# A new order for the head of a two-layer decoder trunk, and another buffer pool for the operands that return at its turn

## The chip, the cores and the metric

One core of one Trainium2 chip runs the whole program. The metric is the device time of one execution in microseconds (us). Before the change the median of three runs is 1879.58 us (1879.56 to 1881.36); one more execution was profiled.

## The reference, cut to what matters

The input x has 2048 rows of 1024 features, p has two layers of 2048 rows of 256. Everything is float32.

```
h = x
for i in (0, 1):
    hn = rmsnorm(h, norm_mix[i])
    if i == 0:                       # gated short convolution, 1024 -> 4 x 1024
        b, c, v, z = split(hn @ a_w_in)
        h += (silu(z) * b * conv3(c * v)) @ a_w_out
    else:                            # gated causal window means over 2, 4, 8, 16 rows
        u, z = split(hn @ b_w_in)
        d = window_means(u) - u      # by groups of 256 features
        h += (silu(z) * (d @ w_grp) * scale) @ b_w_out
    gate = sigmoid(rmsnorm(h, ple_norm[i]) @ ple_w_gate[i])
    h += gate * (p[i] @ ple_w_proj[i])      # the embedding projection
return rmsnorm(h, final_norm)
```

## The kernel before, in words

The rows are cut into four chunks of 512, and features lie on the 128 partitions, eight tiles of 128 by 512 to a chunk. Each float32 factor is split into a high and a low part (the split: a ScalarE cast, line 108 for weights and 240 for operands, and a VectorE subtraction, lines 109 and 241), and each product is three matmuls (lines 212 to 214, `mm`).

Weights come in granules of 128 by 1024 (512 KB). `order` (from line 160) lists all granules in the order of their use; `next_granule` hands out the next one and `prefetch` loads and splits those that lie a few places ahead (one in the head, three later). A granule is loaded into one of four buffers of pool `rawp` and split into one of four buffers of `wring`, or, for p and its projections and the group weights, into two tiles of the token pool `acts` (28 tiles of 128 by 2 by 512). Pool `hp` has ten tiles of 128 by 512 for the chunk that is worked on, pool `wk` ten work tiles for everything short-lived. PSUM has seven banks for products.

The first mixer (`mixer_a`, `pair_steps`) works on two chunks at once with a seven-product scheme in place of eight: its operands x11, x21, t2, t1, t3, x22 and t4, four tiles each, are norms, sums and differences of the two chunks' x. For each output pair of weights it takes x11 and x21 (24 matmuls of 128 by 512), then t2 and t1, then t3 and x22, then t4.

*The head* (from line 725). Some matmuls on constants run first. Then `load_chunk`, `square_sums` and `roots` prepare the norms of chunks 0 and 1, `fold_next` multiplies the group weights into the second mixer's input weights (four folds of 48 matmuls of 128 by 256, stored to DRAM as `wcomb`, each half fold through a buffer of `rawp`), and `ple(0, (0, 1))`, as the last call before the mixer, projects the embeddings of chunks 0 and 1 (96 matmuls) and stores them to DRAM (`p_dram`), from where the gate reads them later.

*The turn.* After the second chunk (`turn`), the mixer needs the operands of chunks 2 and 3. `prepare(kk)` builds those of two feature tiles ahead of time and stores them to DRAM (`n_dram`); the four calls are spread over the work on chunk 1. `second_operand` (line 529) loads one tile back and splits it into the token pool; `Operands.ahead(n)` does so for the next n of the 28.

All loads and stores are issued by SP, in one queue. The program is written in one order, but a planner with its own estimates of durations sets the final order of each engine's instructions: it takes the earliest written one that its estimate finds ready. On the chip each engine then runs its instructions strictly in that order.

Of the kernel before, what the change touches and what calls it, by code (L numbers as in the profile page):

```python
# [9 lines left out]
F32 = mybir.dt.float32  # L10
# [5 lines left out]
P = 128  # L16
D = 1024
S = 2048
T = 512
KT = D // P  # L20
NCH = S // T
# [12 lines left out]
W_GATE = (40, 50)  # L34
W_BZ = 60
W_BOUT = 68
# [11 lines left out]
def trunk_kernel(ctx: ExitStack, tc: tile.TileContext, xT, xN, pT, wts, par, out):  # L48
    nc = tc.nc
# [4 lines left out]
    acts = ctx.enter_context(tc.tile_pool(name="acts", bufs=28))  # L54
    hp = ctx.enter_context(tc.tile_pool(name="hp", bufs=10))
# [8 lines left out]
    def wtile():  # L64
        return wk.tile([P, 528], F32, tag="wk", name="wk")
# [29 lines left out]
    p_dram = {key: dram.tile([P, KT, T], F32, name=f"pdr{key[0]}{key[1]}", tag=f"pdr{key[0]}{key[1]}") for key in PLE_EARLY}  # L95
# [64 lines left out]
    order = []  # L160
# [10 lines left out]
    def ple_order(layer, ch, halves):  # L171
        return [("p", layer * NCH + ch)] + [("pt", W_GATE[layer] + 8 + h) for h in halves]

    for g in range(4):
        order += [("pt", W_GRP + g // 2)] if g % 2 == 0 else []
        order += [("w", W_UT + 2 * g), ("w", W_UT + 2 * g + 1)]
    order += ple_order(0, 0, (0,)) + ple_order(0, 1, (1,))
    for ch in range(NCH):
        if ch % 2 == 0:
            order += [("sum", (0, 0)), ("sum", (1, 0))]  # L180
# [13 lines left out]
    pos = [0]  # L194
    look = [LOOK]

    def prefetch(upto):
        while len(loaded) < len(order) and len(loaded) <= upto:
            loaded.append(load_granule(order[len(loaded)]))

    def next_granule(key):
        prefetch(pos[0] + look[0])
        assert order[pos[0]] == key, (order[pos[0]], key)
        w = loaded[pos[0]]
        pos[0] += 1
        return w


    def mm(ps, w, col, act, first, last, skip=False):
        wh, wl = w[0][:, col:col + P], w[1][:, col:col + P]  # L210
        ah, al = act
        nc.tensor.matmul(out=ps, lhsT=wh, rhs=ah, start=first, stop=False, skip_group_check=skip)  # L212
        nc.tensor.matmul(out=ps, lhsT=wh, rhs=al, start=False, stop=False, skip_group_check=skip)  # L213
        nc.tensor.matmul(out=ps, lhsT=wl, rhs=ah, start=False, stop=last, skip_group_check=skip)  # L214
# [6 lines left out]
    def psum():  # L221
        return pm.tile([P, T], F32, tag="mm", name="mm")
# [154 lines left out]

    def pair_steps(i, X):

        pa, pb = psum(), psum()  # L380
        w = next_granule(("sum", (i, 0)))
        product(pa, w, 0, X("x11"), True)
        product(pb, w, HK, X("x21"), True)
        c1 = copied(pa)
# [142 lines left out]
        nc.sync.dma_start(out=n_dram[kk][:, 5:7, :], in_=b)  # L527

    def second_operand(name, kk):
        n = wtile()[:, :T]  # L530
        nc.sync.dma_start(out=n, in_=n_dram[kk][:, SLOT[name], :])
        return split_act(n)

# [47 lines left out]
    def mixer_out(base, ys, hs, layer, extra=nop):  # L581
        s = Stat()
        a = []
        for k in range(KT):
            ps = dense(("w", base + k), ys)
            nc.vector.tensor_tensor(out=hs[k], in0=ps, in1=hs[k], op=ALU.add)  # L586
            a.append(split_scaled(hs[k], G_PLE + 8 * layer + k))
            s.add(hs[k], nc.vector if k == KT - 1 else nc.gpsimd)
            extra(k)
        return a, s  # L590
# [11 lines left out]
               i == 0, i == 1)  # L602
        return g_ps, p_ps

    def ple(layer, chs):

        pts, wps = {}, []
        base = W_GATE[layer] + 8
        for h in range(2):
            if h < len(chs):  # L610
                pts[chs[h]] = next_granule(("p", layer * NCH + chs[h]))
            wps.append(next_granule(("pt", base + h)))
        for h in range(2):
            for ch in chs:
                pt = pts[ch]
                for k in range(4 * h, 4 * h + 4):
                    ps = psum()
                    for i in range(2):
                        mm(ps, wps[h], ((k % 4) * 2 + i) * P,
                           (pt[0][:, i * T:(i + 1) * T], pt[1][:, i * T:(i + 1) * T]), i == 0, i == 1)  # L620
                    e = wtile()[:, :T]
                    nc.scalar.copy(out=e, in_=ps)
                    nc.sync.dma_start(out=p_dram[layer, ch][:, k, :], in_=e)

    def gate_out(g_ps, p_ps, h, rb, c0, c1):
        t = wtile()[:, :c1 - c0]
# [108 lines left out]
    x, stats = [], []  # L735

    def load_chunk(t):
        x.append([])
        for k in range(KT):
            xt = hp.tile([P, T], F32, tag="h", name="x") if t * KT + k < 10 else wtile()[:, :T]  # L740
            nc.sync.dma_start(out=xt, in_=xT[t, :, k, :])
            x[t].append(xt)

    def square_sums(t):
        s = Stat()
        for k in range(KT):
            s.add(x[t][k], nc.vector)
        stats.append(s)

    def roots(t):  # L750
        stats[t].fin1()
        stats[t].fin2()
# [3 lines left out]
    def fold_next(g):  # L756
        if g % 2 == 0:
            wg.append(next_granule(("pt", W_GRP + g // 2)))
        fold(g, wg[-1], [next_granule(("w", W_UT + 2 * g + c)) for c in range(2)])

    prefetch(2)
    load_chunk(0)
    square_sums(0)
    fold_next(0)
    load_chunk(1)
    roots(0)
    fold_next(1)
    square_sums(1)
    X = Operands(first_operand(x, stats))
    X("x11")  # L770
    fold_next(2)
    roots(1)
    X("x21")
    fold_next(3)
    X("t2")
    ple(0, (0, 1))


    sums_n = const.tile([P, 8], F32, name="sums_n")
    rbs = []  # L780
# [12 lines left out]
    def preparing(kk):  # L793
        return lambda k: prepare(kk, rbs) if k == KT - 1 else None

    for sc in range(2):
        ya = mixer_a(sc, X)
        ys = [split_act(y) for y in ya]
        for t in range(2):
            ch = 2 * sc + t  # L800
            more = ch + 1 < NCH
            turn = (sc, t) == (0, 1)
            hs = load_x(ch)
            a, s = mixer_out(W_AOUT, ys, hs, 0)
            a, s = gate(0, ch, a, hs, s, G_MIX + 8, preparing(1) if turn else nop)
            ys = mixer_b(ch, a, s, gather if ch == 0 else preparing(2) if turn else nop)
            if (1, ch) in PLE_EARLY:
                ple(1, (ch,))
            a, s = mixer_out(W_BOUT, ys, hs, 1, preparing(3) if turn else nop)
            if not more:  # L810
                look[0] = 1
                gate_last(1, ch, a, hs, s)
                break
            nys = []
            if turn:
                X = Operands(second_operand)

            def ahead(k):
                if turn:
                    X.ahead(3 if k < KT - 1 else 2)  # L820
                    return
                nys.append(later_half(sc, k))
                if ch == 0 and k == KT - 1:
                    prepare(0, rbs)

            _, s = gate(1, ch, a, hs, s, None, ahead)
            hooks.extend(finals(ch, hs, s))
            ys = nys
# [53 lines left out]
```

## Time and profile before

| | before |
|---|---|
| median of runs | 1879.58 us |
| profiled execution | 1880.67 us |
| its span | 1878.9 us |
| TensorE busy | 1815.6 us, 97% |
| VectorE busy | 1304.8 us, 69% |
| ScalarE busy | 755.2 us, 40% |
| GpSimd busy | 253.5 us, 13% |
| moved by DMA | 223.75 MB, 119 GB/s in the mean |

All times inside the program are counted from the start of the span. In the profile, PE is TensorE, DVE is VectorE, ACT is ScalarE, POOL is GpSimd and SPq is the queue of SyncE, which issues the transfers. "PEclk" is the granted clock of TensorE, where 1.00 is 2.4 GHz and 0.50 is 1.2 GHz.

### The profile page before, as it was taken

To read this page: it belongs to the slowest core of one execution; us is meant where nothing else is said; L and a number is where in the kernel's file an instruction comes from. 1 tells how busy PE (TensorE), PEld (TensorE's weight loads), DVE (VectorE), ACT (ScalarE), POOL (GpSimd) and SP (SyncE) were. 2 spreads that over 40 slices of the span, in tenths; PEclk is the share of its full clock that TensorE was granted. 3 is DMA by queue.
4 is the path that set the end of the run, shared out by engine and by line. 5 is a ranking of instruction groups with operands and counts; after the bars stand their busy time and mean duration, and the time that the engine had idled before them with its cause. 6 is when DMAs were issued, how large, how long until landed. Compare 5 with 4: busy or idle time off the path is not lost.

```text
span 1878.9 us, 21641 instructions
## 1 busy us (share of the span) xinstructions
PE 1815.6 (97%) x8189; PEld 1503.2 (80%) x8189; DVE 1304.8 (69%) x1791; ACT 755.2 (40%) x1100; POOL 253.5 (13%) x233
## 2 busy tenths in 40 slices
PE   7699999999999999999978999999999999999997
PEld 5587888888888888888856888888888888888897
DVE  7856665765796667896677675666668666768665
ACT  6633333344444434434353233334433344443332
POOL 1000000002221122211110000000222112120010
PEclk7899999999999999999988999999999999999998
DMA  7611111243343455536543111114322343622221
GB/s 252 236 62 64 55 62 62 68 158 123 129 158 123 135 174 191 185 101 207 201 168 113 62 62 62 62 68 162 123 90 90 102 134 113 202 78 92 99 90 45
DMA packets 77272, 223.75 MB, mean 119 GB/s; under 512 B 8560, under 2 KB 10608, under 8 KB 77168
## 3 DMA queue, kind: packets, MB, share of 16 engines
q1 hardware_dynamic: 77168, 222.38, 34.8%
q8 instruction: 64, 1.05, 0.2%
q14 instruction: 40, 0.33, 0.1%
HBM read 191.93 MB, written 30.41 MB: 118 GB/s over the span
## 4 chain that ended last, share of the span: by engine, by line
PE 91%; DVE 3%; DMA 2%; ACT 2%; issue 1%; SPq 0%; POOL 0%; DVEq 0%; ACTq 0%
PE mm L212 30%; PE mm L214 30%; PE mm L213 30%; DVE w L109 1%; DMA wk<-ndr 1%; DMA raw<-in_wts_dram 1%; ACT w L108 1%; DVE act L241 0%; PE tot L280 0%; ACT wc L359 0%; DMA wcomb<-wc 0%; ACT wk L267 0%; DVE h L661 0%; DMA wk<-in_xT_dram 0%; DVE wk L629 0%
## 5 line engine op out<-in xcount | busy, mean ns | idle before, releaser
L212 PE MATMUL mm<-act,w 128*128 128x512 f32 (+1 forms) x2560 | 975.1, 385 | 26.1 <-ACT w L108 8.2
L213 PE MATMUL mm<-act,w 128*128 128x512 f32 (+1 forms) x2560 | 981.6, 384 | 0.2 <-DVE act L241 0.2
L214 PE MATMUL mm<-act,w 128*128 128x512 f32 (+1 forms) x2560 | 966.2, 384 | 3.0 <-DVE w L109 2.9
L212 PEld LDWEIGHTS mm<-act,w 128*128 128x128 f32 x2560 | 487.1, 190 | 129.0 <-ACT w L108 12.1
L108 ACT CAST w<-raw 128x1024 fp32r<-128x1024 f32 (+1 forms) x296 | 296.7, 1006 | 678.5 <-PE mm L214 439.3
L213 PEld LDWEIGHTS mm<-act,w 128*128 128x128 f32 x2560 | 487.0, 190 | 94.2 <-DVE act L241 1.2
L214 PEld LDWEIGHTS mm<-act,w 128*128 128x128 f32 x2560 | 482.0, 189 | 98.6 <-DVE w L109 5.1
L109 DVE TENSOR_TENSOR w<-raw,w 128x1024 fp32r<-128x1024 f32 (+1 forms) x296 | 346.5, 1173 | 130.6 <-ACT w L108 129.8
L270 POOL TENSOR_TENSOR acc<-acc,wk 128x512 f32<-128x512 f32 x97 | 148.9, 1535 | 568.3 <-ACT wk L267 568.0
L375 DVE TENSOR_TENSOR wk<-mm,wk 128x512 f32<-128x512 f32 x96 | 66.0, 689 | 153.7 <-PE mm L214 151.6
L586 DVE TENSOR_TENSOR h<-mm,h 128x512 f32<-128x512 f32 x64 | 43.4, 688 | 80.1 <-PE mm L214 77.0
L247 DVE SCALAR_TENSOR_TENSOR act<-h,par_sb,act 128x512 fp32r<-128x512 f32 x96 | 92.5, 973 | 7.6 <-ACT act L246 7.5
L246 ACT ACTIVATE act<-h,par_sb 128x512 fp32r<-128x512 f32 x96 | 69.1, 719 | 64.7 <-DVE h L630 46.8
L267 ACT ACTIVATE wk<-h 128x512 f32<-128x512 f32 (+1 forms) x119 | 70.9, 596 | 50.9 <-DVE h L630 49.4
L370 ACT COPY wk<-mm 128x512 f32<-128x512 f32 x96 | 52.5, 581 | 88.1 <-PE mm L214 88.1
L240 ACT CAST act<-wk 128x512 fp32r<-128x512 f32 x82 | 49.7, 619 | 69.7 <-DVE wk L577 46.1
L241 DVE TENSOR_TENSOR act<-wk,act 128x512 fp32r<-128x512 f32 x82 | 58.4, 719 | 26.5 <-ACT act L240 26.5
L212 PE MATMUL mm<-act 128*128 128x512 f32 (+1 forms) x144 | 53.5, 374 | 15.3 <-ACT act L108 15.3
L627 DVE TENSOR_TENSOR wk<-mm,rb 128x512 f32<-128x512 f32 (+1 forms) x72 | 44.3, 626 | 34.5 <-PE mm L214 24.8
L423 POOL COPY wk<-uh 128x2 f32<-128x2 f32 x16 | 14.1, 882 | 362.4 <-DVE wk L375 285.6
L109 DVE TENSOR_TENSOR w<-s,w 128x1024 fp32r<-128x1024 f32 x32 | 39.8, 1243 | 28.4 <-ACT w L108 28.2
L560 DVE TENSOR_TENSOR wk<-wk 128x512 f32<-128x512 f32 (+5 forms) x80 | 55.4, 693 | 2.1
(111 smaller groups left out, 1223.0 us busy)
## 6 DMA issues: line engine op xcount, KB each, us to landing
raw<-in_wts_dram SPq DMA_DIRECT2D x252, 512.0 KB, 3.3
raw<-wcomb SPq DMA_DIRECT2D x32, 512.0 KB, 3.3
h<-in_xT_dram SPq DMA_DIRECT2D x32, 256.0 KB, 5.3
wk<-ndr SPq DMA_DIRECT2D x28, 256.0 KB, 4.9
pdr<-wk SPq DMA_DIRECT2D x24, 256.0 KB, 3.1
wk<-pdr SPq DMA_DIRECT2D x24, 256.0 KB, 4.0
out_dram<-h SPq DMA_DIRECT2D x24, 256.0 KB, 2.8
wcomb<-wc SPq DMA_DIRECT2D x16, 256.0 KB, 4.3
```

Of the source, the lines that this page charges most:

```text
L108: nc.scalar.copy(out=hi[:, c], in_=raw[:, c])
L109: eng.tensor_tensor(out=lo[:, c], in0=raw[:, c], in1=hi[:, c].bitcast(F32), op=ALU.subtract)
L212: nc.tensor.matmul(out=ps, lhsT=wh, rhs=ah, start=first, stop=False, skip_group_check=skip)
L213: nc.tensor.matmul(out=ps, lhsT=wh, rhs=al, start=False, stop=False, skip_group_check=skip)
L214: nc.tensor.matmul(out=ps, lhsT=wl, rhs=ah, start=False, stop=last, skip_group_check=skip)
L241: nc.vector.tensor_tensor(out=a[:, 1, :], in0=y, in1=a[:, 0, :].bitcast(F32), op=ALU.subtract)
L246: nc.scalar.activation(out=a[:, 0, :], in_=h, func=AF.Copy, scale=pcol(gcol))
L247: nc.vector.scalar_tensor_tensor(out=a[:, 1, :], in0=h, scalar=pcol(gcol), in1=a[:, 0, :].bitcast(F32), op0=ALU.mult, op1=ALU.subtract)
L267: nc.scalar.activation(out=sq, in_=h, func=AF.Square)
L270: (eng or nc.gpsimd).tensor_tensor(out=acc, in0=acc, in1=sq, op=ALU.add)
L375: nc.vector.tensor_tensor(out=o, in0=ps, in1=c, op=ALU.add)
L560: nc.vector.tensor_tensor(out=nxt[:, lo:end], in0=cur[:, lo:end], in1=cur[:, lo - step:end - step], op=ALU.add)
```

## The change

The head is rewritten: the embedding projections run first, then the four folds and the operands between them. The list of granules is put in the same order. `ple` takes one chunk, and the second call uses the projections of the first again. The second chunk of x is loaded as four transfers of two tiles into the token pool instead of eight transfers into `hp` and `wk`. Loads are called for by `prefetch` at written places.

At the turn, `second_operand` loads into `hp` instead of `wk`. The first four returns are asked for in the stage before (`mixer_out`, tiles 4 to 7), then two in place of three for each tile of the gate. The last `prepare` is called after tile 3 instead of tile 7.

```diff
@@ order
+    order += ple_order(0, 0, (0, 1)) + ple_order(0, 1, ())
     for g in range(4):
         order += [("pt", W_GRP + g // 2)] if g % 2 == 0 else []
         order += [("w", W_UT + 2 * g), ("w", W_UT + 2 * g + 1)]
-    order += ple_order(0, 0, (0,)) + ple_order(0, 1, (1,))
@@ second_operand
-        n = wtile()[:, :T]
+        n = hp.tile([P, T], F32, tag="h", name="nx")
         nc.sync.dma_start(out=n, in_=n_dram[kk][:, SLOT[name], :])
         return split_act(n)
@@ ple
-    def ple(layer, chs):
...
+    def ple(layer, ch, wps=None):
+
+        pt = next_granule(("p", layer * NCH + ch))
+        wps = wps or [next_granule(("pt", W_GATE[layer] + 8 + h)) for h in range(2)]
+        for k in range(KT):
+            ps = psum()
+            for i in range(2):
+                mm(ps, wps[k // 4], ((k % 4) * 2 + i) * P,
+                   (pt[0][:, i * T:(i + 1) * T], pt[1][:, i * T:(i + 1) * T]), i == 0, i == 1)
+            e = wtile()[:, :T]
+            nc.scalar.copy(out=e, in_=ps)
+            nc.sync.dma_start(out=p_dram[layer, ch][:, k, :], in_=e)
+        return wps
@@ load_chunk
-        for k in range(KT):
-            xt = hp.tile([P, T], F32, tag="h", name="x") if t * KT + k < 10 else wtile()[:, :T]
-            nc.sync.dma_start(out=xt, in_=xT[t, :, k, :])
-            x[t].append(xt)
+        for k in range(0, KT, 2):
+            if t == 0:
+                pair = [hp.tile([P, T], F32, tag="h", name="x") for _ in range(2)]
+                for i in range(2):
+                    nc.sync.dma_start(out=pair[i], in_=xT[t, :, k + i, :])
+            else:
+                both = acts.tile([P, 2, T], F32, tag="act", name="x2")
+                nc.sync.dma_start(out=both, in_=xT[t, :, k:k + 2, :])
+                pair = [both[:, i, :] for i in range(2)]
+            x[t].extend(pair)
@@ head
     prefetch(2)
     load_chunk(0)
+    prefetch(3)
     square_sums(0)
-    fold_next(0)
+    ple(0, 1, ple(0, 0))
+    prefetch(6)
     load_chunk(1)
     roots(0)
-    fold_next(1)
+    fold_next(0)
     square_sums(1)
     X = Operands(first_operand(x, stats))
     X("x11")
+    fold_next(1)
+    X("x21")
+    roots(1)
     fold_next(2)
-    roots(1)
-    X("x21")
     fold_next(3)
+    prefetch(pos[0] + 1)
     X("t2")
-    ple(0, (0, 1))
@@ main loop
             if (1, ch) in PLE_EARLY:
-                ple(1, (ch,))
-            a, s = mixer_out(W_BOUT, ys, hs, 1, preparing(3) if turn else nop)
+                ple(1, ch)
+            if turn:
+                X = Operands(second_operand)
+
+            def before(k):
+                if turn and k == 3:
+                    prepare(3, rbs)
+                if turn and k > 3:
+                    X.ahead(1)
+
+            a, s = mixer_out(W_BOUT, ys, hs, 1, before)
...
-            if turn:
-                X = Operands(second_operand)
-
             def ahead(k):
                 if turn:
-                    X.ahead(3 if k < KT - 1 else 2)
+                    X.ahead(2)
                     return
```

## Rows read from the trace of the kernel before

**Rows 1.** The page: share of the span, and 40 slices of it in tenths.
```profile
PE 1815.6 (97%) x8189; PEld 1503.2 (80%) x8189; DVE 1304.8 (69%) x1791; ACT 755.2 (40%) x1100; POOL 253.5 (13%) x233
...
PEclk7899999999999999999988999999999999999998
```

**Rows 2.** Timeline of TensorE in the head: start us, duration us, line, tiles.
```profile
12.84 0.28 PE L212 MATMUL mm<-act,w 128*128 128x256 f32 x1
12.96 0.28 PE L213 MATMUL mm<-act,w 128*128 128x256 f32 x1
...
76.93 0.39 PE L212 MATMUL mm<-act 128*128 128x512 f32 x1
77.16 0.39 PE L213 MATMUL mm<-act 128*128 128x512 f32 x1
...
92.12 0.39 PE L212 MATMUL mm<-act,w 128*128 128x512 f32 x1
```

**Rows 3.** Windows of the head: length, busy us (instructions) by engine, clock, DMA share.
```profile
33.30:45.00 11.70, 9.18 (x41) 8.89 (x42) 11.70 (x18) 6.75 (x14) 0.00 (x0) 0.50 0.23 75
...
6.40:97.10 90.70, 62.53 (x316) 54.76 (x317) 78.47 (x114) 59.99 (x114) 4.44 (x3) 0.79 0.69 239
...
92.10:121.60 29.50, 29.50 (x132) 24.41 (x131) 13.39 (x20) 8.29 (x14) 0.84 (x2) 1.00 0.24 83
```

**Rows 4.** Groups of TensorE by line and shape, 0 to 121.6 us.
```profile
L212 PE MATMUL mm<-act,w 128*128 128x256 f32 x64 | 21.5, 350 | 5.5 <-ACT w L108 4.8 <-ACT wc L359 0.7
```

**Rows 5.** Waits, 0 to 170 us: us in total, times, longest us.
```profile
PE mm L212 <- ACT act L108: 15.3, 1, 15.3
```

**Rows 6.** Windows before and in the turn, columns as in rows 3.
```profile
892.00:957.00 65.00, 65.00 (x288) 53.76 (x287) 46.28 (x62) 27.27 (x40) 11.02 (x7) 1.00 0.56 194
957.00:1030.00 73.00, 54.42 (x193) 41.03 (x192) 54.72 (x83) 29.35 (x48) 7.73 (x8) 0.84 0.39 137
```

**Rows 7.** Waits of TensorE, 880 to 1060 us.
```profile
PE mm L212 <- ACT wk L370: 6.9, 1, 6.9
PE mm L212 <- ACT act L240: 5.9, 2, 4.6
```

**Rows 8.** Timeline of VectorE: the last operand splits of the head.
```profile
95.14 1.89 DVE L241 TENSOR_TENSOR act<-x,act 128x512 fp32r<-128x512 f32 x3
```

**Rows 9.** Waits of SP's queue, 0 to 100 us.
```profile
SPq L102 <- DMA wcomb<-wc: 10.1, 4, 4.3
```

**Rows 10.** Timeline of SP's queue in the turn.
```profile
973.42 0.32 SPq L643 DMA_DIRECT2D wk<-pdr  x1
...
992.61 0.33 SPq L102 DMA_DIRECT2D raw<-in_wts_dram  x1
992.99 2.32 SPq L531 DMA_DIRECT2D wk<-ndr  x5
```

**Rows 11.** Timeline of ScalarE in the turn.
```profile
982.01 0.63 ACT L267 ACTIVATE wk<-h 128x512 f32<-128x512 f32 x1 [2.39 <-DVE h L630]
982.54 1.05 ACT L370 COPY wk<-mm 128x512 f32<-128x512 f32 x2
```

**Rows 12.** The page: costliest groups (busy, mean ns), then transfers (count, KB, us to landing).
```profile
L108 ACT CAST w<-raw 128x1024 fp32r<-128x1024 f32 (+1 forms) x296 | 296.7, 1006 | 678.5 <-PE mm L214 439.3
L109 DVE TENSOR_TENSOR w<-raw,w 128x1024 fp32r<-128x1024 f32 (+1 forms) x296 | 346.5, 1173 | 130.6 <-ACT w L108 129.8
L240 ACT CAST act<-wk 128x512 fp32r<-128x512 f32 x82 | 49.7, 619 | 69.7 <-DVE wk L577 46.1
L241 DVE TENSOR_TENSOR act<-wk,act 128x512 fp32r<-128x512 f32 x82 | 58.4, 719 | 26.5 <-ACT act L240 26.5
...
raw<-in_wts_dram SPq DMA_DIRECT2D x252, 512.0 KB, 3.3
...
wk<-ndr SPq DMA_DIRECT2D x28, 256.0 KB, 4.9
```

**Rows 13.** Waits of SP's queue, 900 to 1030 us.
```profile
SPq L102 <- DVE w L109: 75.4, 11, 16.0
```

More of the change, by code (lines that the diff above doesn't have):

```diff
@@ L603, in gate_mm @@
         return g_ps, p_ps
-    def ple(layer, chs):
[L607 to L623, printed above, removed]
+    def ple(layer, ch, wps=None):
[10 more added lines that the diff above has]
+        return wps
     def gate_out(g_ps, p_ps, h, rb, c0, c1):
```

## The prediction, on record before the changed kernel ran

> **What bounds the kernel now.** I read the busy shares first, then the row of 40 slices, then the causes of TensorE's idle time, then the two stretches that they point to. TensorE is busy 97% of the span, and its granted clock is full but for the first slices and one place in the middle [rows 1]. So the kernel is a stream of matmuls, 0.2267 us from the start of one 128x512 matmul to the next (76.93 to 77.16 and on, [rows 2]), and a change can only win where that stream is broken: in the head (0 to 92 us) and at the turn between the halves of the sequence (957 to 1030 us). The diff touches just these.
>
> Head. The mixer's first matmul runs at 92.12 us [rows 2], and behind it the stream is whole: 29.5 us from there hold 29.50 us of busy TensorE [rows 3]. Before it TensorE has 192 fold matmuls (64 on each of three lines, [rows 4]) at 0.12 us (12.84 to 12.96, [rows 2]), 23.0 us; 96 embedding matmuls (2 chunks x 8 tiles x 2 halves x 3) at 0.2267, 21.8 us; and some 1.4 us of statistics, 46.2 us in all. The first fold starts at 7.7 us, so an unbroken head would end at 53.9 us: 38.2 us are lost. The largest piece is one wait of 15.3 us [rows 5], for the cast of an embedding granule, which stands behind the folds and finds no early slot; the others are 3 to 4 us each. The rest is clock: from 33.3 to 45 us, after such gaps, the granted clock is 0.50 [rows 3], the 1.2 GHz level.
>
> Turn. A full stream records 288 matmuls in 65 us (892 to 957); the 73 us behind it hold 193 where 323 would fit [rows 6]. The missing 130, at 65/288 = 0.226 us, are 29.3 us lost, 18.6 us of it idle (73 less 54.42) and the rest a lower clock (0.84 in the mean). Two waits of TensorE lead: 6.9 us for a PSUM copy, 5.9 us for operand casts [rows 7].
>
> **The change, part by part.**
>
> Order of the head. The embeddings come first and need only p and its projections, so TensorE can start at the same 7.7 us: the first three granules have the size of those that stood there. 21.8 us of matmuls, and some 1.5 us for a half clock at the start as the first fold had it, lead to 31 us; beside them run the casts of the fold weights, the squares of x and the first roots. The 15.3 us wait goes, since its granules are the first loaded. Late next is VectorE. From 6.4 to 97.1 us it was busy 78.5 us, 87% [rows 3], and its last operand splits end at 97.0 [rows 8]. None of that work is removed: granule splits, 14 square adds, norms, sums, 28 operand splits. The last operand, t4, is wanted 96 matmuls after the mixer's first (two steps of 24 on x11 and x21, then 12 each on t2, t1, t3, x22), 21.8 us later. If VectorE never waits, t4 is done at 6.4 + 78.5 = 84.9 and the mixer can start, in effect, at 63.1 us, a gain of 29 us. At the old 87%, t4 stays at 97.0 and the start is 75.2, a gain of 17. I take the middle, 69 us, since granule work now covers VectorE's early waits for x while the roots' chain through TensorE and GpSimd stays: gain 23 us. The lower bound: the folds now stand directly in front of the mixer, and each half fold keeps one of four raw buffers until its store has landed, for which weight loads already stood 10.1 us on SP [rows 9]. If that is paid in full on top of the old 87%, the gain is 7 us. The DMA engines were 69% busy in the same stretch [rows 3]; at full load its bytes take 63 us, to 69 us, no later than VectorE.
>
> Loads of x. Chunk 1 comes as four transfers of 512 KB in place of eight of 256 KB, in the token pool of 28 in place of pools h and wk, which leaves all ten work tiles to the embeddings' evictions. These 16 stores move to the front of SP's queue, ahead of fold weights: at 0.32 to 0.46 us an issue (as SP's rows show, [rows 10]) 5 to 7 us, hidden under 21.8 us of embedding matmuls. Without that cover the fold waits those 7 us; four fewer loads give 1.5 us back at best. I take nothing for both.
>
> The turn. The returning operands leave the work tiles, for which the gate's temporaries and its embedding tiles compete. The gate's last embedding tile was loaded only at 973.42 us [rows 10], 16 us into the stretch that should hold the mixer, and the PSUM copy for which TensorE waited 6.9 us ran on ScalarE at 982.54 behind a square that itself waited for the gate's tail [rows 11]. With this competition gone, and x11 fetched one stage ahead, I expect both waits to go, 12.8 us, with half of the 10.7 us of lower clock, 5: 17.8 us. Against it stand the new buffers. Pool h has ten, eight hold the chunk, so two returns fly at a time. One takes 4.9 us to land, 0.62 us of cast and 0.72 us of subtraction [rows 12], 6.24 us, so 3.12 us a return. Twenty of 28 can be back before the gate's own operands free the token pool: from 893 us that is 955 us, in time. The last eight (x22, t4) need four rounds, 25 us, to 980 and beyond, where before five came in one burst at 992.99 [rows 10]. They are wanted from 19 us after the mixer's start at 957 on, 976 to 979; the burst's replacement is then some 8 us late and I take that in full: net gain 10 us. Bounds: 29 us gained if nothing is left of the loss; if the 17.8 do not come and two rounds more are waited for, 12 us lost.
>
> Preparing the fourth operand pair at tile 3 in place of 7 moves two loads, eight VectorE passes and four stores into a stretch in which VectorE is busy 46 of 65 us [rows 6]. It leaves the way between the last sum and the root, but TensorE did not stop for that root: nothing; under 1 us either way, a pass at the most. The projection of the second layer issues what it issued: nothing.
>
> Sum: 1880.7 us (span 1878.9 and 1.8 around it) - 23 - 10 = 1847.7; the profiled run lies 1.1 us above the median of the runs, so 1847 us beside them.
>
> **Rivals.** (1) VectorE gives the head back. For it: it is 87% busy over the whole head. Against: in the old order the mixer began 5 us before the last split was ready, 17 us later than it need have. Head 7, turn 3 gained: 1870 us. (2) Two buffers starve the turn: 3.12 us a return is above the 2.72 us (12 matmuls) at which two per gate tile are asked, and any queueing on VectorE adds to each round. Against: x11 starts a stage earlier. Head 23 gained, turn 5 lost: 1862 us. (3) Slower: SP's one queue at the turn. A return that waits for its buffer stands before the weight loads. SP already stood up to 16.0 us for a weight buffer [rows 13], and the five returns behind that load were issued 0.4 us after it, at 992.99 [rows 10]. If a tile's two returns must first free a buffer and the next weights land only after, a tile takes 6.2 us and 5.5 us more (landing 3.3, cast 1.0, split 1.2, [rows 12]), 11.7 in place of 5.44 us: 50 us on eight tiles, less 16 us that three granules of look-ahead cover, 34 us lost. With a head of 23 and none of the 10 it ends at 1892 us. It decides from the point where a buffer wait exceeds 5.44 us a tile; against it, 3.12 us a return is near the pace asked. The Trainium skill (DMA: Bandwidth & Descriptors, Anatomy of one DMA) says that DMA engines wait on no semaphore and that any such wait is on the issuing sequencer, before dispatch; by that rule this queueing is certain wherever a buffer is late, and the 0.4 us above agrees. (4) The planner, which orders each queue by its own estimate of times, gives the written order away and the moved lines issue where they did: 1880 us.
>
> **How the numbers follow.** Forecast 0.58, own range 1836 to 1859; rival 1, 0.18; rival 2, 0.11; rival 3, 0.08; rival 4, 0.05. About 0.2% (3.8 us) is what a measurement of this kernel tells from no change. Faster: forecast and rivals 1 and 2, 0.87; same 0.05; slower 0.08. The range of 8 in 10 takes in rival 2, most of rival 1 and a little of a turn that loses nothing more: 1834 to 1872.
>
> **What would show it.** The first embedding matmul at 7.7 us; no idle TensorE above 5 us before the mixer; its first matmul between 58 and 75 us, with some gaps behind it put down to VectorE (t2, t1, t4). At the turn no wait for the PSUM copy, the gate's embedding loads 5.4 us apart, and short waits for casts at x22 and t4. I am wrong if the mixer starts as early as that but TensorE then idles over 15 us for splits, or if SP's weight loads wait on buffers of h.

## The result, and the profile after

The changed kernel takes 1857.37 us (median of 4 runs, 1856.24 to 1859.52) beside 1879.57 us of the kernel before on the same chip: a ratio of 0.9882, 95% interval 0.9865 to 0.9899, so 22.2 us are gained where 33 were forecast. Its profiled execution has 1859.5 us and a span of 1857.7.

To see where the 21.2 us of span come from I align the two traces on an instruction that both have: ScalarE's copy of the row factor for a later norm. Lines of its timeline (start us, duration us, engine and line, tiles, idle before and releaser), the kernel before, then after:

```profile
463.72 0.59 ACT L303 COPY rb<-bc 128x512 f32<-128x512 f32 x1 [1.86 <-PE bc L301]
...
1352.88 0.59 ACT L303 COPY rb<-bc 128x512 f32<-128x512 f32 x1 [0.27 <-PE bc L301]
```

```profile
458.88 0.59 ACT L303 COPY rb<-bc 128x512 f32<-128x512 f32 x1 [1.86 <-PE bc L301]
...
1332.01 0.59 ACT L303 COPY rb<-bc 128x512 f32<-128x512 f32 x1 [0.27 <-PE bc L301]
```

The first pair lies behind the head and before the turn, the second behind both. The changed kernel is 4.84 us ahead at the first and 20.87 at the second. So **the head gained 4.8 us and the turn 16.0**, where I had written 23 and 10. Below, "head" and "turn" of a run are these two differences against the kernel before. They come from one execution each: two heads of the same code differ by up to 2 us (4.84 here, 6.68 in e7, which has the same head).

From the page of the changed kernel, the granted clock in 40 slices of the span:

```profile
PEclk9889999999999999999999999999999999999998
```

The dip of the clock in the middle is gone, the one at the start has only become smaller [rows 1]. The head in windows, columns as in [rows 3], and the turn's window as in [rows 6]:

```profile
6.40:65.00 58.60, 47.73 (x256) 41.70 (x257) 41.26 (x57) 42.90 (x81) 4.02 (x3) 0.91 0.77 283
65.00:105.00 40.00, 26.64 (x112) 21.63 (x111) 39.79 (x61) 21.98 (x40) 0.00 (x0) 0.79 0.44 141
17.50:40.50 23.00, 23.00 (x135) 20.30 (x133) 13.27 (x18) 18.11 (x35) 1.65 (x1) 1.00 0.97 361
957.00:1030.00 73.00, 65.64 (x270) 52.90 (x269) 57.30 (x83) 26.82 (x41) 9.14 (x9) 0.93 0.31 106
```

and the same first two stretches of the kernel before:

```profile
6.40:65.00 58.60, 33.91 (x198) 31.24 (x198) 48.90 (x72) 34.64 (x71) 3.78 (x2) 0.74 0.74 253
65.00:105.00 40.00, 36.52 (x153) 30.09 (x154) 32.27 (x47) 27.61 (x47) 0.66 (x1) 0.91 0.53 185
```

Read TensorE (first figure) against VectorE (third). Up to 65 us TensorE does 13.8 us more than before (47.73 less 33.91), and VectorE 7.6 us less (48.90 less 41.26). From 65 to 105 us VectorE has no gap left (39.79 of 40) and TensorE loses 9.9 us of its lead. The timeline of TensorE in the changed kernel shows where:

```profile
21.47 0.39 PE L280 MATMUL tot<-acc_hi,ones_r 128*128 128x512 f32 x1
...
31.70 0.39 PE L280 MATMUL tot<-acc_lo,ones_r 128*128 128x512 f32 x1
...
74.92 0.63 PE L212 MATMUL mm<-act,w 128*128 128x512 f32 x1
...
92.99 0.79 PE L212 MATMUL mm<-act,w 128*128 128x512 f32 x1 [6.42 <-ACT w L108]
...
98.00 0.80 PE L214 MATMUL mm<-act,w 128*128 128x512 f32 x1 [2.94 <-DVE w L109]
```

The 15.3 us wait [rows 5] is gone, and the mixer's first matmul stands at 74.92, 17.2 us earlier than at 92.12 [rows 2]. Of these 17.2 us 12.4 are given back behind it: 9.4 us in the two waits for weight granules, and most of the rest at 1.2 GHz beside them (from 98.5 to 103.4 us the granted clock is 0.50, and a matmul starts 0.43 us after the one before in place of 0.227). Why the weights are late stands in the queues of the two engines that make them, VectorE first:

```profile
32.19 0.69 DVE L286 TENSOR_TENSOR wk<-tot,fold 128x512 f32<-128x512 f32 x1 [2.90 <-PE tot L280]
...
87.70 0.68 DVE L134 TENSOR_TENSOR s<-s,raw 128x512 f32<-128x512 f32 x1
...
92.52 4.29 DVE L241 TENSOR_TENSOR act<-x,act 128x512 fp32r<-128x512 f32 x7
96.73 1.21 DVE L109 TENSOR_TENSOR w<-s,w 128x1024 fp32r<-128x1024 f32 x1
...
99.60 2.49 DVE L241 TENSOR_TENSOR act<-x,act 128x512 fp32r<-128x512 f32 x4
```

```profile
86.01 5.98 ACT L240 CAST act<-x 128x512 fp32r<-128x512 f32 x11 [0.69 <-DVE x L484]
91.89 1.04 ACT L108 CAST w<-s 128x1024 fp32r<-128x1024 f32 x1
```

The granule that TensorE waits for at 92 us is a sum of weights. VectorE ends that sum at 88.4 us (L134), between work on operands. Its cast then stands on ScalarE behind the rest of eleven operand casts (6 us in all), and its remainder on VectorE behind seven operand splits (4.3 us): both queues are in order. VectorE's backlog ends with the last splits at 102.1 us, 5.1 us later than the 97.0 of before [rows 8], although it has the same work (1791 instructions and 1307.0 us in the whole kernel, 1304.8 before). It was starved at the front: the second of the two matmuls that sum root 0 runs at 31.70, ten us after the first, since the queue of TensorE has embedding matmuls between them; its operand acc_lo was ready at 19.4. The row factor of chunk 0 follows, and only then can its norms begin. ScalarE's copy of it, the kernel before, then after:

```profile
30.91 0.58 ACT L303 COPY rb<-bc 128x512 f32<-128x512 f32 x1
```

```profile
39.91 0.59 ACT L303 COPY rb<-bc 128x512 f32<-128x512 f32 x1 [0.32 <-PE bc L301]
```

It comes nine us later, and that of chunk 1 eleven (64.45 in place of 53.59). Not all of VectorE's idle time is a wait for them: its longest wait behind 7 us, 4.0 us up to 28.06, is for the cast of a fold weight. What the late root costs is read from e2.

The turn: TensorE's waits from 957 to 1030 us (us in total, times, longest), and SP's for a returning operand from 880 to 1000 us.

```profile
PE mm L212 <- ACT wk L370: 4.8, 1, 4.8
```

```profile
SPq L531 <- DVE act L241: 29.2, 25, 2.5
```

```profile
L531 SPq DMA_DIRECT2D nx<-ndr x26: 319/319/320, 894.1 to 965.3; - x26
...
DMA to landing us min/median/max: 2.5/3.2/4.9
```

The returns (the last fence: count, duration in ns, first and last start) begin at 894.1 us and go out one by one as a buffer comes free, up to 965.3; each lands in 3.2 us (median).

The window holds 270 matmuls where 193 stood [rows 6], so 53 of 323 are missing, 12.0 us at 0.226, not 29.3. Of the 17.3 us between, 11.2 are idle time (65.64 us busy against 54.42), the rest is clock. The wait for operand casts [rows 7] is gone, that for the PSUM copy is down from 6.9 to 4.8, and one of 2.2 us for a square of the gate (L267) is new. A third wait is gone that the prediction had not counted. In the kernel before, TensorE waits 4.1 us for an add that VectorE does at 1021.95 us, behind eight passes of the final norm:

```profile
PE mm L212 <- DVE wk L375: 4.1, 1, 4.1
```

```profile
1015.38 5.38 DVE L661 SCALAR_TENSOR_TENSOR h<-h,par_sb,rb 128x512 f32<-128x512 f32 x8
```

In the changed kernel the planner has put these passes elsewhere (they start at 1004.78, behind three such adds), and no wait of this kind is left.

### The profile page after: what moved, and what is told of

Its sections match the earlier page's. It is cut to its first block, busy times and chain, and to the rows that moved or that the text cites. A ratio compares the mean times of both kernels' runs of the same rounds, so it can differ in the third digit from the quotient of the medians.

```text
span 1857.7 us, 21624 instructions
## 1 busy us (share of the span) xinstructions
PE 1808.7 (97%) x8189; PEld 1499.4 (81%) x8189; DVE 1307.0 (70%) x1791; ACT 758.3 (41%) x1100; POOL 252.5 (14%) x233
## 4 chain that ended last, share of the span: by engine, by line
PE 91%; DVE 4%; DMA 2%; ACT 1%; issue 1%; SPq 0%; POOL 0%; DVEq 0%; ACTq 0%
PE mm L212 30%; PE mm L214 30%; PE mm L213 30%; DVE act L241 1%; DMA nx<-ndr 1%; DVE w L109 1%; DMA raw<-in_wts_dram 1%; DVE x L484 0%; DMA wk<-pdr 0%; ACT w L108 0%; DVE x L481 0%; PE tot L280 0%; DVE o L695 0%; ACT wk L267 0%; ACT act L240 0%
## 5 line engine op out<-in xcount | busy, mean ns | idle before, releaser
L212 PE MATMUL mm<-act,w 128*128 128x512 f32 (+1 forms) x2560 | 973.7, 384 | 20.8 <-ACT w L108 12.4
L214 PEld LDWEIGHTS mm<-act,w 128*128 128x128 f32 x2560 | 482.4, 189 | 106.2 <-DVE w L109 12.4
L370 ACT COPY wk<-mm 128x512 f32<-128x512 f32 x96 | 52.6, 582 | 93.0 <-PE mm L214 92.9
L267 ACT ACTIVATE wk<-h 128x512 f32<-128x512 f32 (+1 forms) x119 | 70.9, 596 | 44.8 <-DVE h L624 42.3
L291 POOL TENSOR_TENSOR r<-ms,nhalf 128x8 f32<-128x8 f32 x17 | 29.8, 1753 | 193.5 <-DVE ms L289 193.5
L212 PE MATMUL mm<-act 128*128 128x512 f32 (+1 forms) x144 | 53.3, 373 | 2.6 <-ACT act L108 2.6
L213 PE MATMUL mm<-act 128*128 128x512 f32 (+1 forms) x144 | 53.7, 373 | 0.0
```

What stands on the lines that cost most here:

```text
L267: nc.scalar.activation(out=sq, in_=h, func=AF.Square)
L370: nc.scalar.copy(out=c, in_=ps)
```

## The experiments

"After" is the changed kernel. Each run is timed against the kernel before on its own chip; ratios have their 95% interval.

**e1: the turn alone.** The kernel before, with only the part of the change that the turn has.

```diff
-        n = wtile()[:, :T]
+        n = hp.tile([P, T], F32, tag="h", name="nx")
...
+                if turn and k == 3:
+                    prepare(3, rbs)
+                if turn and k > 3:
+                    X.ahead(1)
...
-                    X.ahead(3 if k < KT - 1 else 2)
+                    X.ahead(2)
```

> The old head with the new turn. The two traces, aligned on the copies of the row factors, put 4.8 us of the gain into the head and 16.0 into the turn. If the two parts don't act on each other: 1879.6 - 16 = 1863.5 us, and the copies before the turn stand where they stood before the change. Rival: the turn gains only because the head shifted the plan behind it; then the turn alone gains under 8 us, above 1871 us.

Measured: 1865.48 us, 0.9916 (0.9901 to 0.9931); head -0.6, turn 15.1. The two parts add up: 15.1 and 4.8 make 19.9 of the 20.9. So the small gain of the head is the head's own doing, not a cost of the turn's edits.

**e4: the embedding tiles of the head stored twice.** After, with 4.2 MB more to write in the first 40 us.

```diff
             nc.sync.dma_start(out=p_dram[layer, ch][:, k, :], in_=e)
+            if layer == 0:
+                nc.sync.dma_start(out=p_twice[ch][:, k, :], in_=e)
```

> The changed kernel, with each of the head's sixteen embedding tiles stored a second time to a place that nobody reads: 4.2 MB more among the loads of the first 40 us, where the DMA engines already run at 97 to 102% of their time. Theory C (the stores that came to the front push chunk 1 and the fold weights back): 4.2 MB at the 400 GB/s of this stretch are 10.5 us, so the head loses 5 to 10 us against the change, 1862 to 1867 us. Theory A or B (VectorE's order and the raw buffers decide): under 3 us lost, 1857 to 1860 us.

Measured: 1863.69 us, 0.9912 (0.9897 to 0.9927); head 0.8, turn 14.7. The time lies in theory C's range, the 4.0 us that the head lost are a little under it. TensorE's timeline has a long wait in the second of the four folds, where after waits 2.7 and 1.8 us, and then the mixer's first matmul:

```profile
49.95 0.58 PE L213 MATMUL mm<-act,w 128*128 128x256 f32 x1 [10.54 <-ACT w L109]
...
78.92 0.40 PE L213 MATMUL mm<-act,w 128*128 128x512 f32 x1
```

The DMA engines were already 97% busy from 17.5 to 40.5 us in after, and 4.2 MB at the 0.39 MB a us that they move there in this run are 10.8 us. Of these only 4.0 us reach the mixer's start (78.92 in place of 74.92), and the same 4.0 reach the end of the head. So the transfers at the front are not free, and they don't set the end either: six of ten us are covered inside the folds, by the 4.5 us that after waits at the same place and by later waits that get shorter, and nothing more is covered behind them.

**e2: root 0 ahead of the second embedding chunk.** After, with one line moved.

```diff
-    ple(0, 1, ple(0, 0))
+    wps = ple(0, 0)
+    roots(0)
+    ple(0, 1, wps)
...
-    roots(0)
```

> The changed kernel, with the first chunk's root written between the two embedding calls instead of behind both, so that its second matmul runs some 7 us sooner on TensorE. Theory A (VectorE is idle 17 us before 65 us, since norms wait for roots, and is the bound from there to 102 us): x11 is normed some 7 us sooner, the head gains 4 to 7 us more than the change's 4.8, 1851 to 1853 us. Theory B (the folds' raw buffers set the mixer's start): within 1 us of the change. Theory C (the DMA engines are full for the first 40 us, and chunk 1 comes late): root 0 is not what is late, within 2 us of the change.

Measured: 1847.88 us, 0.9824 (0.9809 to 0.9839); head 16.4, turn 16.5. The head gains 11.6 us on after, about twice what I expected. The second sum of root 0 runs at 23.54 in place of 31.70, the mixer starts 10.9 us earlier than in after:

```profile
23.54 0.39 PE L280 MATMUL tot<-acc_lo,ones_r 128*128 128x512 f32 x1
...
64.03 0.39 PE L212 MATMUL mm<-act,w 128*128 128x512 f32 x1
```

```profile
6.40:65.00 58.60, 50.94 (x298) 44.95 (x298) 46.04 (x64) 46.58 (x91) 3.43 (x3) 0.94 0.85 309
```

VectorE has 4.8 us more done by 65 us (46.04 against 41.26) and is full behind it again (39.7 of the 40 us up to 105). So one line moved gives back more than twice what the whole head of the change had won.

**e3: both roots ahead of the folds.** After, with chunk 1 of x loaded ahead of the embeddings and both roots before the first fold.

```diff
+    load_chunk(1)
     square_sums(0)
-    ple(0, 1, ple(0, 0))
+    wps = ple(0, 0)
+    roots(0)
+    square_sums(1)
+    ple(0, 1, wps)
+    roots(1)
     prefetch(6)
...
```

> The changed kernel, with chunk 1 loaded before the embeddings and both roots written between and right behind the embedding calls. Theory A: both norms are known some 10 to 20 us sooner, VectorE fills its idle time, the head gains 10 to 15 us more, 1842 to 1848 us. Theory B: the folds still end at 75 us and the mixer starts there; under 4 us more. Theory C: chunk 1's loads now delay the fold weights instead; 0 to 6 us more, and the fold starts later than 32 us.

Measured: 1851.12 us, 0.9841 (0.9826 to 0.9855); head 14.3, turn 15.7: 9.4 us on after, a little less than expected. Its window up to 65 us and the waits of TensorE:

```profile
6.40:65.00 58.60, 50.06 (x287) 44.26 (x288) 49.72 (x71) 43.29 (x82) 3.92 (x3) 0.94 0.86 308
```

```profile
83.75 0.79 PE L212 MATMUL mm<-act,w 128*128 128x512 f32 x1 [5.12 <-ACT w L108]
...
88.76 0.79 PE L214 MATMUL mm<-act,w 128*128 128x512 f32 x1 [2.93 <-DVE w L109]
```

VectorE is fed best of all (49.72), its last splits end at 92.9, nine us earlier than in after. But the same two waits for weights stand in TensorE's queue: the granules are still behind the operand casts. So feeding VectorE earlier does not take these waits away: the order in the queues is a matter of its own.

**e5: the folds' results in the token pool.** After, with the results of a half fold held in the token pool until they are stored, and no longer in the four raw buffers, in which weight loads stood behind them.

```diff
-            both = rawp.tile([P, 2, 4, P], F32, tag="raw", name="wc")
+            both = acts.tile([P, 2, 4, P], F32, tag="act", name="wc")
```

> The changed kernel, with the folds' results in the token pool instead of the raw buffers, so that no weight load waits for a store. Theory B: the folds end at 60 us or so in place of 75 and the head gains 8 to 12 us more, 1845 to 1849 us. Theory A: the folds end sooner, but the mixer then waits longer for VectorE; under 3 us more. Theory C: under 3 us.

Measured: 1847.30 us, 0.9823 (0.9806 to 0.9839); head 18.1, turn 15.8; 13.2 us on after's head, just above what theory B had given (8 to 12) and far from the under 3 us of the other two. So the raw buffers were a cost of the new head too. With e2 it is the fastest of the runs that leave no work out, and beats both kernels. In after, weight loads stood on SP for the landing of a fold's store (first 105 us; us in total, times, longest); here they don't:

```profile
SPq L102 <- DMA wcomb<-wc: 4.1, 3, 2.5
```

The mixer starts at 63.87 us. TensorE's longest wait behind that, and VectorE's last operand splits:

```profile
79.86 0.50 PE L212 MATMUL mm<-act,w 128*128 128x512 f32 x1 [4.66 <-ACT act L240]
...
102.42 1.28 DVE L241 TENSOR_TENSOR act<-x,act 128x512 fp32r<-128x512 f32 x2
```

```profile
6.40:65.00 58.60, 52.08 (x298) 46.52 (x299) 45.93 (x63) 47.58 (x91) 4.21 (x3) 0.91 0.96 346
63.87:103.70 39.83, 31.91 (x129) 24.39 (x128) 39.73 (x63) 20.26 (x33) 0.00 (x0) 0.91 0.27 88
```

Weights load early enough here for their casts to be done before the operands'; TensorE's longest wait is for an operand. VectorE is ahead by 4.7 us at 65 us and full behind it, as in e2. So the two edits, on different resources, come to about the same place.

**e9: e2 and e5 together.**

> Both edits that gave the head back its gain: the root of chunk 0 between the embedding calls, and the folds' results in the token pool. Each alone brought the mixer's first matmul from 74.9 to 64 us, with 11.6 and 13.2 us more gain. If they are two ways out of one wait (weight splits late behind norms, and then raw buffers late), together they give hardly more than the better one, 1844 to 1848 us. If they are two costs of their own, the mixer starts near 55 us, the unbroken end of embeddings and folds, and the time is 1836 to 1841 us.

Measured: 1849.39 us, 0.9833 (0.9816 to 0.9849); head 14.4, turn 16.1. That is in neither range. They don't add; the head is 2 to 4 us behind either of them, which is little more than two executions of one head differ.

```profile
59.76 0.40 PE L212 MATMUL mm<-act,w 128*128 128x512 f32 x1
...
83.24 1.22 PE L212 MATMUL mm<-act,w 128*128 128x512 f32 x2 [12.15 <-ACT act L240]
```

Here TensorE comes to the mixer almost unbroken at 59.8 us, the earliest of all, and then stands for operands, 12.2 us in the wait above and 3.7 in one at 88.1. They need the row factor of chunk 1, which comes at 70.56 us, later than in e2 (60.63) and e5 (67.73). So a start made earlier on TensorE alone is given back.

**e10, e11, e13: VectorE's work given to GpSimd.** On e5: the adds of the squares of chunk 1 (e10), or the twelve operand subtractions of t3, x22 and t4 (e11). On e2: the same twelve (e13).

```diff
-            s.add(x[t][k], nc.vector)
+            s.add(x[t][k], nc.gpsimd if t else nc.vector)
...
-        nc.vector.tensor_tensor(out=a[:, 1, :], in0=y, in1=a[:, 0, :].bitcast(F32), op=ALU.subtract)
+        eng.tensor_tensor(out=a[:, 1, :], in0=y, in1=a[:, 0, :].bitcast(F32), op=ALU.subtract)
...
+            return split_act({"t3": n12, "x22": n22, "t4": n21}[name], nc.gpsimd)
```

> The kernel with the folds' results in the token pool (18.0 us of head), with the square sums of chunk 1 added on GpSimd instead of VectorE: 7 additions, 4.3 us, leave VectorE, while GpSimd has hardly any work in the head. If VectorE's total work now sets the head's end: 3 to 4 us less, 1843 to 1844 us. If the root of chunk 1 is what is late (GpSimd takes 1.5 us an addition, 11 us for a chunk), it gets later by 4 to 7 us and the time is 1850 us or more.

> The same kernel, with the subtractions of the twelve splits of t3, x22 and t4 in the head on GpSimd instead of VectorE: 7.2 us leave the stretch from 65 to 102 us in which VectorE is never idle, and GpSimd takes some 18 us for them beside it. If VectorE's work in this stretch sets the head's end: 4 to 7 us less, 1840 to 1843 us. If not (weights or stores set it): within 2 us of 1847. If GpSimd becomes late for t3: 1850 us or more.

> The kernel with the root of chunk 0 between the embedding calls (16.4 us of head), with the same twelve subtractions on GpSimd. VectorE theory as in the run before it: 4 to 7 us less than 1847.9, 1841 to 1844 us; otherwise within 2 us of 1848.

Measured: 1851.93 us, 0.9856 (0.9839 to 0.9872), head 10.6; 1854.11, 0.9873 (0.9858 to 0.9888), head 10.0; 1854.80, 0.9877 (0.9862 to 0.9891), head 10.2. All three are slower than the kernels they stand on. GpSimd's and VectorE's timelines of e11:

```profile
92.26 19.76 POOL L241 TENSOR_TENSOR act<-x,act 128x512 fp32r<-128x512 f32 x12 [32.94 <-DVE act L241]
```

```profile
101.02 1.76 DVE L133 TENSOR_TENSOR s<-raw 128x512 f32<-128x512 f32 x1
```

GpSimd takes 1.65 us in the mean for a subtraction that VectorE does in 0.6, one after the other up to 112 us, and VectorE's add beside it takes 1.76 where the same line took 0.68 in after. The work was made longer, not only moved, so e11 and e13 tell nothing of whether VectorE sets the end. e10 fell into its second range, and as that range had it: the row factor of chunk 1 comes at 73.42 us in place of 67.73 in e5, and TensorE's longest wait for an operand grows from 4.7 to 8.0 us. So on e5 the root of chunk 1 is on the path, as far as one run tells. Whether VectorE's work is, is seen better where it shrinks:

**e14: part of VectorE's work left out.** After, without the sixteen sums and differences that make t2, t1, t3 and t4.

```diff
-                vec(n12, n22, n12, ALU.subtract)
-                vec(n11, n12, n11, ALU.add)
                 return split_act(n11)
             if name == "t1":
-                vec(n21, n21, n11, ALU.subtract)
-                vec(n11, n22, n11, ALU.subtract)
```

> The changed kernel, with the sixteen sums and differences that form t2, t1, t3 and t4 of the first two chunks left out (the splits take what lies in the tiles): 16 x 0.60 us, 9.6 us, leave VectorE between 70 and 88 us and go to no other engine. VectorE theory (from 65 to 102 us VectorE is never idle, and the weight splits that TensorE waits for stand in its queue behind operands): TensorE's waits of 6.4 and 2.9 us and their half clock shrink, the head gains 6 to 10 us more, 1847 to 1851 us. Raw buffer theory (weights come late because the stores of the folds hold the buffers): the folds still end at 75 us and the same waits stay, within 2 us of 1857.

Measured: 1848.15 us, 0.9823 (0.9806 to 0.9839); head 15.9, turn 16.5: 11.0 us on after, for 9.6 us of VectorE's passes.

```profile
77.49 0.62 PE L212 MATMUL mm<-act,w 128*128 128x512 f32 x1
```

```profile
54.56 3.68 DVE L241 TENSOR_TENSOR act<-x,act 128x512 fp32r<-128x512 f32 x6
...
81.50 2.49 DVE L241 TENSOR_TENSOR act<-x,act 128x512 fp32r<-128x512 f32 x4
84.53 0.69 DVE L133 TENSOR_TENSOR s<-raw 128x512 f32<-128x512 f32 x1 [0.55 <-DMA raw<-in_wts_dram]
```

```profile
65.00:105.00 40.00, 36.01 (x178) 30.80 (x177) 31.68 (x46) 21.26 (x42) 0.19 (x1) 0.96 0.46 163
```

The mixer starts 2.6 us later than in after, and the head still ends 11 us sooner: the splits are done at 84 us, VectorE has 8.3 of the 40 us free, and behind the mixer's start TensorE waits for nothing up to 135 us. The weights themselves come no sooner: VectorE begins the sum of the granule at 84.53, when its load lands, and began it at 84.69 in after. So the two waits of after are time in which weights stand behind operands in the two queues, and not late loads. The edit does more than shorten VectorE's work, though: without the sums t2 and t1 no longer need chunk 1's row factor, and 16 of the 28 splits are done by 65 us where after has 8. No run separates the two. Nor does the end of VectorE's work alone set the head's end: e5 has its last split at 103.7 us, later than after, and the better head.

**e7: the early start, the old buffers.** After, with the returning operands in work tiles again.

```diff
-        n = hp.tile([P, T], F32, tag="h", name="nx")
+        n = wtile()[:, :T]
```

> The changed kernel, with the returning operands in the work tiles again, but still asked for one stage ahead and two to a tile. Theory P (the pool decides, since returns and the gate's temporaries share ten work tiles): most of the turn's 16 us is lost again, 1867 to 1873 us. Theory Q (the early start decides: 20 of 28 are back before the stage ends, whichever pool they pass): under 4 us lost, 1857 to 1862 us. The head keeps its 4.8 us in both.

Measured: 1863.16 us, 0.9908 (0.9893 to 0.9923); head 6.7, turn 11.2.

**e8: the new buffers, the old start.** The kernel before, with the opposite of that line alone.

> The kernel before, with only the pool of the returning operands changed: three to a gate tile, none a stage ahead, the last preparation after tile 7. Theory P: most of the turn's gain of 15 us (as the turn alone gave it) comes with this one line, 1865 to 1869 us. Theory Q: two buffers at the 2.6 us a return that the changed kernel shows need 73 us for 28 returns from 927 on, to 1000 us, so that the mixer waits for t3, x22 and t4: within 5 us of the kernel before or slower, 1876 to 1890 us.

Measured: 1865.65 us, 0.9922 (0.9907 to 0.9937); head -0.7, turn 15.3. That is in theory P's range for e8, while e7 lies between the ranges of P and Q. Waits of TensorE from 957 to 1030 us in e7, then in e8:

```profile
PE mm L212 <- DVE wk L375: 4.1, 1, 4.1
PE mm L212 <- ACT wk L370: 2.9, 1, 2.9
PE mm L212 <- ACT act L240: 2.8, 1, 2.8
```

```profile
PE mm L212 <- ACT wk L370: 7.5, 1, 7.5
```

The early start alone brings 11.2, the buffers alone 15.3, both 16.0 (15.1 in e1). Neither the theory that the pool gives the gain nor the one that the early start gives it holds: each alone gives most of it, and not by the same waits. The early start alone halves the waits for operand casts (2.8 in place of 5.9 us [rows 7]) and that for the PSUM copy (2.9), but leaves the 4.1 us behind the passes of the final norm. The buffers alone end those for casts and the 4.1, and leave that for the PSUM copy (7.5). The burst of five returns at 992.99 [rows 10] is gone in both (in e8 the returns go out from 920.1 to 989.6, one by one), but in the kernel before only 2.5 us of TensorE's waits in this window stood between it and the 4.1. With the pool line there, the early start is worth no more than two executions differ.

## Why the prediction was right or wrong

**The sum** came out on the right side and inside the range because two terms missed in opposite directions: the head was put 18 us too high, the turn 6 too low. That is luck: with the turn as forecast the time would have been some 1863 us, outside the forecast's own range of 1836 to 1859.

**The head: "I take the middle, 69 us".** This is the step that failed, the term of 23; 4.8 was measured, less than the lower bound of 7. Its argument was "since granule work now covers VectorE's early waits for x". It does not: VectorE's idle time before 65 us grew from 9.7 us to 17.3 (58.6 less the busy figures above), because the change put the matmuls of root 0 behind embedding matmuls in TensorE's in-order queue. e2, which only moves them ahead of those of the second chunk, gives 4.8 of these 7.6 us back, and 11.6 us of head. My two ends were a VectorE that never waits and one that waits as before; that the new order could make it wait more, I did not price. By my own rule (the mixer starts, in effect, 21.8 us before the last split) a last split at 102.1 gives a start of 80.3 and a gain of 11.8; the other 7 us are the weights queued behind operands on ScalarE and VectorE. That rule was itself too strict: in e5 the last split ends at 103.7, 40 us behind the mixer's first matmul, and the head is 13 us better: TensorE does 129 matmuls in between, where I had counted 96, so it works on steps whose operands are there. Rival 1, "VectorE gives the head back", had the mechanism and, with 7 us, nearly the size; e14 bears it out as far as it goes. Its turn of 3 did not come. The lower bound had a second cause that the middle left out, half folds that keep raw buffers until their store has landed; e5 takes it away and the head gains 13.2 us. Either cause out of the way gives most of what there is, and both together (e9) no more.

How the 11.6 and 13.2 us of e2 and e5 divide between a VectorE fed earlier (4.8 and 4.7 us by 65 us) and a better order in the queues, no run separated; e3, which is fed 8.5 us better and gains 9.4, shows only that the first does not rank them alone. That stays open.

**"No idle TensorE above 5 us before the mixer"** held: the longest was 4.0 us. The start at 74.9 lies at the end of the 58 to 75 us given, and the sign that I had named for being wrong, over 15 us of idle TensorE for splits behind it, appeared in part: 9.4 us of idle, put down to weights that wait in the splits' queue.

**"I take nothing" for the stores and loads of x** held for the end of the head, not for the way there. From 17.5 to 40.5 us the DMA engines are full (97%), and e4 shows that 10.8 us of bytes added there cost the mixer's start, and the head, 4.0. In e5 and e2, where TensorE waits less in the folds, I did not measure that price again.

**The turn: "some 8 us late and I take that in full".** This term was not there. By the prediction's own figures the last return comes at 980 us and is wanted at 976 to 979, which is 1 to 4 us late and not 8. And it assumed 4.9 us a landing, from transfers sent up to five at a time; sent one by one they land in 3.2, and the last goes out at 965.3 and so lands near 968.5, some 10 us ahead of the 979 (the mixer itself starts some 5 us earlier). Rivals 2 and 3 needed a return to stand over 5.44 us on SP: the longest stood 2.5. The Trainium skill (DMA: Bandwidth & Descriptors, Anatomy of one DMA) says that a DMA's wait is taken on the issuing sequencer; the 25 waits on SP, 29.2 us in total, agree. At 1.2 us each the queue behind them did not feel it: TensorE's waits for weights in the window add up to 0.3 us. Of the 12.8 us of waits that I expected to go, the 5.9 for casts went, and of the 6.9 for the PSUM copy 4.8 stayed: it still stands behind a square that waits for the gate's tail, as in [rows 11], only 10.6 us earlier (971.95 in place of 982.54). The 4.1 us behind the final norm went unforeseen. With 12.0 of 29.3 us of loss left, 17.3 went in that window, where I had counted 17.8 before the 8: nearly the size, in part by another wait.

**Rival 4**, that the planner gives the old order back, fell with the first matmuls: the embeddings run at 8 us, where the folds did.

## What to carry to other kernels

When work moves away from a late wait, what it was queued ahead of moves too: find the engine that is full until the end of the stretch (here VectorE), follow back to the first thing that its long work needs (here a row factor), and look where the instructions that make it will now stand in each in-order queue, and what they and the weights behind them must wait for (here buffers held by stores). Ask of a new order whether it can make that engine wait more than now; the profile before bounds only how long it waits in the old one. To see which part of a change paid, align both traces on one instruction between the parts.

## What the runs showed of the hardware

From 17.5 to 40.5 us the DMA engines of one core moved 361 GB/s in after, at 97% busy, and 397 in e5 (at 104%, since a transfer counts in full where it starts). The four 512 KB loads of x landed there in 7.6 us (median, after), where the 512 KB weight loads of the whole kernel land in 3.3 [rows 12]:

```profile
x<-in_xT_dram SPq DMA_DIRECT2D x4, 512.0 KB, 7.6
```

GpSimd's 1.65 us (mean of 12, 1.28 to 2.32, e11) for a 128x512 subtraction, and what it does to its neighbour, I had not expected either. In e11 VectorE's add of two SBUF tiles took 1.76 us, while its add of a PSUM and an SBUF tile, beside the same GpSimd work 1.7 us later, kept 0.68:

```profile
102.70 0.68 DVE L375 TENSOR_TENSOR wk<-mm,wk 128x512 f32<-128x512 f32 x1
```

The Trainium skill (GPSIMD Engine Reference, Specifications) says that GpSimd shares its SBUF interface with VectorE and that they contend where VectorE's instruction has two SBUF inputs; these two rows agree, and give the price.
